# Two batches of small matmuls in an RWKV chain write to another PSUM bank of a two-layer hybrid decoder kernel

## The chip, the cores and the metric

The kernel runs on one core of one Trainium2 chip. The metric is the device time in microseconds of one execution, lower is better. Times of three runs are given, and one further execution was profiled; all views of the trace are of that one.

## The reference, cut to what matters

Two layers of a decoder trunk on 512 tokens of width 1024, in float32. Each layer normalises x, multiplies it by one large matrix, and hands the columns to three token mixers: latent attention (MLA), attention with a forget gate (FOX), and RWKV-7. Their outputs are gated, projected, merged and projected once more.

```python
for l in range(DEPTH):
    h = rmsnorm(x, norm_g[l])
    p = h @ w_in[l]
    (c_q, c_kv, k_r, gate_a, fq, fk, fv, ff, gate_b, shift_cols, gate_c, merge_cols) = split_cols(p, IN_SIZES)
    o_a = mla_branch(c_q, c_kv, k_r, gate_a, ...)
    o_b = fox_branch(fq, fk, fv, ff, gate_b, ...)
    r, k, v, wl, al = split_cols(shifted, RWKV_SIZES)
    o_c = rwkv_branch(r, k, v, wl, al, gate_c, ...)
    merged = sigmoid(g_a)*(o_a @ w_pa[l]) + sigmoid(g_b)*(o_b @ w_pb[l]) + sigmoid(g_c)*(o_c @ w_pc[l])
    x = x + merged @ w_out[l]

def rwkv7_scan(r, w, k, v, kk, a):      # per head, state S is 64 x 64
    sa = einsum('bhvk,bhk->bhv', state, -kk_t)
    state = state * w_t + sa * (kk_t * a_t) + v_t * k_t
    y_t = einsum('bhvk,bhk->bhv', state, r_t)
```

## The kernel before

**The dense part.** A projection is 8 blocks of 128 rows of weights against h. Weights and h are each split into a high and a low part, so a block is three matmuls of 128x512 (`mm3`, lines 816 to 818) and a projection 24, all adding up in one PSUM bank with the tag `acc`. A weight block comes by DMA (`raw`), ACT or DVE copies its high part (line 684), and DVE or POOL subtracts to get the low part (line 696).

**The PSUM banks.** There are eight: three for `acc`, two for `wk` (attention scores and small products of the attention's preparation), and one each for `xk`, `ch` and `av`. The preparation of an RWKV head pair uses `xk`, and `ch` beside it for the products called At. The RWKV chain of a pair uses `ch`. The attention's values use `av`.

**RWKV.** The recurrence is computed in chunks of 64 tokens, for four head pairs per layer, so eight times in the kernel. For each pair:

- The preparation ends with a sum over heads in `xk` (lines 712 and 713) that DVE turns into `bv` (line 1012). Then come two halves of At: 8 matmuls of 64x128 each (line 1018, 16 rows in the trace), alternately into `xk` and `ch`, and after each half two DVE products with a mask (line 1022) that empty the two banks. Then an inverse is built, partly on POOL, and ends with two rounds of small matmuls in `xk` (lines 1061 and 1067).
- The chain takes four batches of 64x64 blocks, written by the helper `one` (line 1099). The first, called here **the M batch**, alternates between R in `ch` and M in `xk`. The second, **the T batch**, alternates between U in `ch` and T in `xk`; it reads R and M, which ACT or DVE copied from PSUM in between. Two more batches in `ch` follow, then six dependent steps of the state (line 1139 on PE, line 1140 on DVE), and the output (lines 1146 and 1150).

**What sets the order.** Five generators per layer emit the work: `p` (RWKV preparation), `c` (RWKV chain), `y` (attention), `z` (merge gates) and `m` (merge). `weave` takes steps from them in a given order; a generator that yields "wait" lets another go first. A function `plan` then lists the emitted instructions engine by engine, with costs and due times, and that list is the order on the chip: each engine works through its own list in that order. `kernel` plans several times, with random shifts of the due times, and keeps the plan with the lowest score. So an edit in one place can move instructions everywhere.

**The rule for banks.** Tiles of one tag take its banks in the order in which they were emitted. `plan` puts the first instruction of a tile behind the first instruction of the tile emitted before it, and behind the last use of the tile that had the bank:

```python
        for x, y in zip(ns, ns[1:]):
            if uses[x][0] < uses[y][0]:
                ops[uses[y][0]].after.setdefault(uses[x][0], False)
        for x, y in zip(ns, ns[slots[tag]:]):
            for k in uses[x]:
                if k < uses[y][0]:
                    successors[k].append(uses[y][0])
```

A projection is emitted only while fewer than three `acc` tiles are open (`open_`).

Of the kernel before, what the change touches and what calls it, by code (L numbers as in the profile page):

```python
# [79 lines left out]

BUFS = {"tx": 8, "ty": 4, "sm": 1, "pp": 2, "raw": 4, "w": 6}
MB = ["wk", "wk", "av", "xk", "ch", "wk", "av", "xk"]
MARGINS = (1.7, 1.5)
SLACK = 1.2
WIRE, AHEAD = 250, 1500
ROUNDS = 3
WINDOW = 3413
SEARCH, JITTER = 12, 2000
PB = {"acc": 3, "wk": 2, "xk": 1, "ch": 1, "av": 1}
DRY = {"raw": 4, "w": 6, "acc": 1}  # L90

# [480 lines left out]
def build(tc, x_t, wpk, wsm, wv, vec, cst, out, order_of=None, pick={}, queues=None, margin=2.0):  # L572
    dry = order_of is None
# [34 lines left out]
    def PS(tag, z=""):  # L608
        b = PB[tag]
        if dry and tag == "acc":  # L610
            b, tag = DRY["acc"], tag + z
        return psum.tile([128, 512], F32, name=tag, tag=tag, bufs=b)
# [12 lines left out]
    def beside(insts):  # L625

        for a, b in zip(insts, insts[1:]):
            order(b, a)
# [6 lines left out]
    def size(ap):  # L635
        return math.prod(q[1] for q in ap.ap[1:])
# [33 lines left out]
    def any_of(costs, emit):  # L670

        key = (stream[0], turn[stream[0]])
        turn[stream[0]] += 1
        q = pick.get(key, costs[0][0])
        flex[emit(q).ins.name] = (key, costs)

    def in_psum(ap):
        return tags[ap.tensor.name][0] == "ps"

    def copy(dst, src, first=ACT):  # L680
        n, p = size(src), in_psum(src)
        costs = [(ACT, (52 if p else 94) + 0.833 * n), (DVE, 68 + n / (0.96 if p else 1.92))]
        any_of(costs if first == ACT else costs[::-1],
               lambda q: act.activation(dst, src, AF.Copy) if q == ACT else dve.tensor_copy(dst, src))  # L684

    def fill(dst, v):
        n = size(dst)
        any_of([(POOL, 34 + 0.836 * n), (DVE, 8 + n / 0.96)], lambda q: (dve if q == DVE else gp).memset(dst, v))
# [73 lines left out]
    for l in range(L):  # L762
# [57 lines left out]
        open_ = [0]  # L820
# [251 lines left out]
        def rwkv_chain(p, ops):  # L1072
# [25 lines left out]
            chunks = lambda tag="ch": PS(tag).rearrange("p (c t) -> p c t", t=64)  # L1098
# [5 lines left out]
                for h, hs in enumerate(HS):  # L1104
                    copy(KT[SH[h], i:8:2, :], ps[es, :, hs])
            yield
            pr, pm = chunks(), chunks("xk")
            beside([one(*a) for c in range(8) for h in range(2) for a in
                    ((pr[SH[h], c, :], At[HS[h], h, c, 0:64], VSA[HS[h], c, HS[h]]),
                     (pm[SH[h], c, :], W[SH[h], c, :], KT[SH[h], c, :]))])  # L1110
            copy(R, pr)
            copy(M, pm)
            yield
            pu, pt = chunks(), chunks("xk")
            beside([one(*a) for c in range(8) for h in range(2) for a in
                    ((pu[SH[h], c, :], W[SH[h], c, :], R[SH[h], c, :]),
                     (pt[HS[h], c, :], M[SH[h], c, :], KBn[SH[h], c, HS[h]]))])
# [7 lines left out]
            for h, hs in enumerate(HS):  # L1125
                fill(KBn[hs, :, SH[h]], 0.0)
                dve.tensor_tensor(KBn[hs, :, hs], pt[hs], C["ident"][hs, hs].unsqueeze(1).broadcast_to([64, 8, 64]),
                                  op=ALU.add)
            yield
            ps = chunks()  # L1130
            for c in range(8):
# [61 lines left out]
        def rwkv_chains():  # L1193
            for p in range(4):
                while len(ready) <= p:
                    yield "wait"
                yield from rwkv_chain(p, ready[p])
                done[0] += 1
# [602 lines left out]
```

## Time and profile before

| | |
|---|---|
| three runs | 1364.81 us median, 1363.15 to 1365.7 |
| the profiled execution, its own time | 1366.35 us |
| its span, first to last instruction | 1364.6 us |
| granted TensorE clock, mean | 0.996 of full speed |
| busy: PE, DVE, ACT, POOL | 97%, 78%, 68%, 30% of the span |
| PE idle | 1364.6 - 1318.9 = 45.7 us |

PE is TensorE, PEld its weight loads, DVE VectorE, ACT ScalarE, POOL GpSimd. A matmul's row shows its whole passage through the array, about 0.40 us for 128x512, while the next may start 0.23 us after it; so a PE that is "busy" can still be waiting a little between starts, and the idle time is only the part of the waiting that shows.

### The profile page before, as it was taken

The numbers are of one execution on the slowest core, as the hardware profiler recorded it, in microseconds if no ns is written. First come the engines' busy times: TensorE is split into PE (matmuls) and PEld (weight loads), VectorE is DVE, ScalarE is ACT, GpSimd is POOL, SyncE is SP. The second block draws the span as 40 slices with busy tenths as digits, with TensorE's granted clock in tenths as the row PEclk, the third lists the DMA queues.
The fourth block names the chain that finished last, engine by engine and source line by source line (L and its number), as shares of the span: only waits on it lengthen the run. The fifth ranks groups of instructions, "written<-read, shape, count | busy, mean of one in ns | idle before, by whom it ended". The sixth has DMA issues, their size and how long they took to land.

```text
span 1364.6 us, 25008 instructions
## 1 busy us (share of the span) xinstructions
PE 1318.9 (97%) x8532; PEld 1049.0 (77%) x8532; DVE 1070.8 (78%) x2430; ACT 934.5 (68%) x1905; POOL 407.5 (30%) x794
## 2 busy tenths in 40 slices
PE   7999999999999999999999999999999999999998
PEld 6777778878777887688877777777776777777787
DVE  8867887788897777977788689878887688848883
ACT  8658677676877775854556767766787588857631
POOL 1245443116211611320021443531254043503210
PEclk9999999999999999999999999999999989999999
DMA  5443233233232342465535333323234333334662
GB/s 176 131 130 103 95 95 92 73 120 102 75 120 75 120 125 71 150 191 180 174 90 164 99 103 100 104 82 91 81 92 107 98 94 106 93 117 124 194 218 97
DMA packets 114623, 158.67 MB, mean 116 GB/s; under 512 B 36544, under 2 KB 44608, under 8 KB 114496
## 3 DMA queue, kind: packets, MB, share of 16 engines
q1 hardware_dynamic: 114496, 157.08, 38.0%
q8 instruction: 67, 1.10, 0.3%
q14 instruction: 60, 0.49, 0.1%
HBM read 128.72 MB, written 28.31 MB: 115 GB/s over the span
## 4 chain that ended last, share of the span: by engine, by line
PE 71%; DVE 15%; ACT 11%; issue 3%; DMA 0%; SPq 0%; DVEq 0%; ACTq 0%
PE acc L817 16%; PE acc L816 16%; PE acc L818 16%; PE wk L1248 3%; PE ch L1099 2%; DVE w L696 2%; ACT w L684 1%; PE av L1260 1%; PE av L1262 1%; DVE qk L684 1%; PE wk L816 1%; PE av L1261 1%; DVE PP L696 1%; PE xk L1018 1%; PE wk L818 1%
## 5 line engine op out<-in xcount | busy, mean ns | idle before, releaser
L816 PE MATMUL acc<-hh,w 128*128 128x512 f32 x1008 | 374.4, 404 | 16.1 <-ACT hh L684 9.0
L818 PE MATMUL acc<-hh,w 128*128 128x512 f32 x1008 | 370.8, 403 | 2.8 <-DVE w L696 2.8
L817 PE MATMUL acc<-hl,w 128*128 128x512 f32 x1008 | 369.7, 402 | 1.3 <-DVE hl L696 1.1
L684 ACT ACTIVATE w<-raw 128x256 fp32r<-128x256 f32 (+1 forms) x544 | 216.6, 412 | 199.1 <-PE acc L818 162.7
L696 DVE TENSOR_TENSOR w<-raw,w 128x256 fp32r<-128x256 f32 x569 | 245.5, 444 | 73.4 <-ACT w L684 69.1
L816 PEld LDWEIGHTS acc<-hh,w 128*128 128x128 f32 x1008 | 189.1, 190 | 60.5 <-ACT hh L684 9.9
L696 POOL TENSOR_TENSOR w<-raw,w 128x256 fp32r<-128x256 f32 (+1 forms) x131 | 116.4, 895 | 399.5 <-ACT w L684 251.8
L818 PEld LDWEIGHTS acc<-hh,w 128*128 128x128 f32 x1008 | 188.7, 189 | 42.6 <-DVE w L696 4.8
L817 PEld LDWEIGHTS acc<-hl,w 128*128 128x128 f32 x1008 | 189.3, 189 | 41.1 <-DVE hl L696 3.1
L1041 POOL TENSOR_TENSOR W<-W,NL 128x60 f32<-128x60 f32 (+24 forms) x248 | 87.6, 353 | 83.4 <-DMA NL<-d 53.0
L1043 POOL TENSOR_TENSOR W<-W 128x60 f32<-128x60 f32 (+24 forms) x248 | 94.2, 380 | 18.1
L1248 PE MATMUL wk<-qk 96*128 96x512 f32 (+9 forms) x320 | 95.8, 319 | 3.5 <-DVE PP L696 2.4
L696 DVE TENSOR_TENSOR PP<-wk,PP 128x512 fp32r<-128x512 f32 (+3 forms) x128 | 61.0, 484 | 17.0 <-ACT PP L684 16.1
L1248 PEld LDWEIGHTS wk<-qk 128*128 128x128 f32 (+2 forms) x320 | 59.9, 189 | 17.5 <-DVE PP L696 6.6
L684 DVE CAST w<-raw 128x256 fp32r<-128x256 f32 (+1 forms) x156 | 46.9, 307 | 31.2 <-PE acc L818 26.0
L1223 DVE CUSTOM_DVE_ANT_0 wk<-wk,cmask 128x128 f32<-128x128 f32 (+3 forms) x128 | 61.4, 498 | 6.2 <-PE wk L1222 5.6
L684 ACT ACTIVATE PP<-wk 128x512 fp32r<-128x512 f32 (+3 forms) x122 | 52.0, 435 | 9.8 <-PE av L1262 5.9
L1249 DVE TENSOR_TENSOR wk<-wk,dmask 128x128 f32<-128x128 f32 x128 | 37.1, 292 | 21.9 <-PE wk L1248 21.3
L1253 ACT ACTIVATE wk<-wk,ncum 128x512 f32<-128x512 f32 (+1 forms) x64 | 31.3, 494 | 21.6 <-DVE wk L1249 21.4
L1253 ACT ACTIVATE wk<-wk 128x512 f32<-128x512 f32 (+1 forms) x64 | 26.9, 423 | 27.9 <-DVE wk L1249 27.4
L817 PE MATMUL acc<-mKR,w 128*128 128x512 f32 x128 | 46.0, 397 | 0.0
L684 ACT ACTIVATE KV<-ch 64x256 f32<-64x256 f32 (+2 forms) x65 | 32.7, 503 | 18.0 <-PE ch L1150 10.7
(532 smaller groups left out, 2872.2 us busy)
## 6 DMA issues: line engine op xcount, KB each, us to landing
raw<-wpk SPq DMA_DIRECT2D x326, 256.0 KB, 2.7
thd<-zth SPq DMA_DIRECT2D x48, 256.0 KB, 2.1
tx<-thd SPq DMA_DIRECT2D x44, 256.0 KB, 3.4
tx<-odr SPq DMA_DIRECT2D x22, 256.0 KB, 3.8
raw<-wpk SPq DMA_DIRECT2D x32, 128.0 KB, 2.2
NL<-d SPq DMA_DIRECT2D x32, 128.0 KB, 2.9
odr<-sg SPq DMA_DIRECT2D x14, 256.0 KB, 2.4
sum<-thd SPq DMA_DIRECT2D x10, 256.0 KB, 2.8
```

Of the source, the lines that this page charges most:

```text
L684: lambda q: act.activation(dst, src, AF.Copy) if q == ACT else dve.tensor_copy(dst, src))
L696: any_of(costs, lambda q: (dve if q == DVE else gp).tensor_tensor(dst, a, b, op=op))
L816: pe.matmul(ps, wh, xh, start=first, stop=False)
L817: pe.matmul(ps, wh, xl, start=False, stop=False)
L818: pe.matmul(ps, wl, xh, start=False, stop=last)
L1041: gp.tensor_tensor(tv, WL[:, 0:m, s:s + 1].broadcast_to([128, m, n]), NL[:, s:s + 1, s + 1:32].broadcast_to([128, m, n]), op=ALU.mult)
L1043: gp.tensor_tensor(WL[:, 0:m, s + 1:32], WL[:, 0:m, s + 1:32], tv, op=ALU.add)
L1099: one = lambda *a: pe.matmul(*a, start=True, stop=True)
L1223: dve.tensor_tensor_reduce(out=ps[:, 0:n], in0=ps[:, 0:n], in1=cmask[:, 512 - n:512], scale=1.0, scalar=NEG, op0=ALU.add, op1=ALU.max, acc ...
L1248: pe.matmul(pv, t[rows, k, js], t[rows, q, q0:512], start=i == 0, stop=i == len(passes) - 1)
L1249: dve.tensor_tensor(ps[:, js], ps[:, js], dmask, op=ALU.add)
L1253: act.activation(pv, pv, AF.Exp, scale=A["scale"], bias=b)
```

## The change

The M tile and the T tile move from the bank `xk` to the ring of three `acc` banks. The chain counts each as an open `acc` tile (`open_`), and waits at emission while three are open. The planner's list of margins gets a third entry, and each planning makes 8 random attempts in place of 12.

```diff
-MARGINS = (1.7, 1.5)
+MARGINS = (1.5, 1.7, 1.5)
...
-SEARCH, JITTER = 12, 2000
+SEARCH, JITTER = 8, 2000
...
-            pr, pm = chunks(), chunks("xk")
+            while not dry and open_[0] >= PB["acc"]:
+                yield "wait"
+            open_[0] += 1
+            pr, pm = chunks(), PS("acc", "c").rearrange("p (c t) -> p c t", t=64)
             beside([one(*a) for c in range(8) for h in range(2) for a in
                     ((pr[SH[h], c, :], At[HS[h], h, c, 0:64], VSA[HS[h], c, HS[h]]),
                      (pm[SH[h], c, :], W[SH[h], c, :], KT[SH[h], c, :]))])
             copy(R, pr)
             copy(M, pm)
+            open_[0] -= 1
             yield
-            pu, pt = chunks(), chunks("xk")
+            while not dry and open_[0] >= PB["acc"]:
+                yield "wait"
+            open_[0] += 1
+            pu, pt = chunks(), PS("acc", "c").rearrange("p (c t) -> p c t", t=64)
...
+            open_[0] -= 1
             yield
```

The program has 7092 matmuls before and after. The new plan lists them in another order from the first projections on. Two places are shown, both of the third head pair of the second layer, on PE. The names are those of the tiles, with their numbers; every `acc` tile read from `hh` or `hl` is a projection, `wk` tiles written at line 1222 (line 1230 in the changed file) are attention scores.

The first place, before: the end of the M batch (`ch_12845`, `xk_12846`) and the start of the T batch (`ch_12886`, `xk_12887`).

```order
L1099 MATMUL ch_12845<-KV_12592,At_11290 64x64
L1099 MATMUL xk_12846<-KR_11254,W_11997 64x64
L712 MATMUL wk_13193<-PP_13194,bd_95 128x512
L816 MATMUL acc_13352<-hh_7485,w_13355 128x512
L713 MATMUL wk_13193<-PP_13194,bd_95 128x512
L817 MATMUL acc_13352<-hl_7486,w_13355 128x512
L816 MATMUL acc_13376<-hh_7485,w_13379 128x512
L818 MATMUL acc_13352<-hh_7485,w_13355 128x512
L817 MATMUL acc_13376<-hl_7486,w_13379 128x512
L1099 MATMUL ch_12886<-At_11290,W_11997 64x64
L1099 MATMUL xk_12887<-KV_12592,At_11290 64x64
```

Five projection matmuls and two of a sum stand between the two batches.

The same place in the changed kernel: the M batch is `ch_12692` and `acc_12693`, the T batch `ch_12750` and `acc_12751`. The first rows are the scores before the M batch, the last ones the first projections after the T batch.

```order
L1230 MATMUL wk_12744<-qk1_12513 128x384
L1230 MATMUL wk_12747<-qk1_12513 128x512
L1099 MATMUL ch_12692<-KV_12165,At_11306 64x64
L1099 MATMUL acc_12693<-KR_11273,W_11706 64x64
...
L1099 MATMUL ch_12750<-At_11306,W_11706 64x64
L1099 MATMUL acc_12751<-KV_12165,At_11306 64x64
...
L816 MATMUL acc_12815<-hh_7485,w_12818 128x512
L816 MATMUL acc_12844<-hh_7485,w_12847 128x512
L817 MATMUL acc_12815<-hl_7486,w_12818 128x512
```

The T batch follows the M batch with nothing between, and no projection starts before the T batch has. (The left-out rows are the rest of the two batches.)

The second place, before: from the sum that feeds `bv` (`xk_11263`) to the first half of At (`xk_11291`, `ch_11292`).

```order
L713 MATMUL xk_11263<-PP_11264,bd_95 128x512
L817 MATMUL acc_11571<-hl_7486,w_11574 128x512
L1262 MATMUL av_11303<-PP_11348,Vh_9231 128x128
L818 MATMUL acc_11571<-hh_7485,w_11574 128x512
L816 MATMUL acc_11571<-hh_7485,w_11592 128x512
L1222 MATMUL wk_11429<-qk1_8177 128x256
L1222 MATMUL wk_11432<-qk1_8177 128x384
L817 MATMUL acc_11571<-hl_7486,w_11592 128x512
L1018 MATMUL xk_11291<-KR_11254,KB0_11253 128x128
L1018 MATMUL ch_11292<-KR_11254,KB0_11253 128x128
```

Four projection matmuls, two scores and one product of the values stand between.

The same place in the changed kernel, which here runs on into the rows of the first place: the sum is `xk_12491`, the halves are `xk_12533` with `ch_12534` and `xk_12545` with `ch_12546`.

```order
L818 MATMUL acc_12416<-hh_7485,w_12475 128x512
L713 MATMUL xk_12491<-PP_12492,bd_95 128x512
L1230 MATMUL wk_12668<-qk0_12379 128x256
L1230 MATMUL wk_12689<-qk0_12379 128x384
L1230 MATMUL wk_12728<-qk0_12379 128x512
L1018 MATMUL xk_12533<-KR_12482,KB0_12481 128x128
L1018 MATMUL ch_12534<-KR_12482,KB0_12481 128x128
...
L1230 MATMUL wk_12738<-qk1_12513 128x128
L1230 MATMUL wk_12741<-qk1_12513 128x256
L1018 MATMUL xk_12545<-KR_12482,KB0_12481 128x128
L1018 MATMUL ch_12546<-KR_12482,KB0_12481 128x128
```

The row of `acc_12416` is the last of that projection and the last of any until `acc_12815`: the sum, both halves of At, the M batch and the T batch stand in one stretch with scores alone between them.

## Rows read from the trace of the kernel before

**Rows 1.** The page, its first part: busy us, share of the span, instructions.

```profile
PE 1318.9 (97%) x8532; PEld 1049.0 (77%) x8532; DVE 1070.8 (78%) x2430; ACT 934.5 (68%) x1905; POOL 407.5 (30%) x794
```

**Rows 2.** The page, the chain that ended last: shares of the span by engine.

```profile
PE 71%; DVE 15%; ACT 11%; issue 3%; DMA 0%; SPq 0%; DVEq 0%; ACTq 0%
```

**Rows 3.** Windows of the span: busy us (instructions) by engine, granted clock, DMA share, GB/s.

```profile
536.10:584.80 48.70, 45.61 (x261) 35.69 (x261) 42.92 (x99) 34.77 (x70) 14.62 (x15) 1.00 0.41 130
1218.40:1267.10 48.70, 46.20 (x284) 36.49 (x281) 41.12 (x95) 33.65 (x68) 16.40 (x15) 1.00 0.40 123
```

**Rows 4.** Line 1099, 1209.3 to 1216.8 us: duration ns min/median/max, first and last start.

```profile
L1099 PE MATMUL ch<-KV,At x32: 218/218/267, 1209.4 to 1210.4; 64*64 64x64 f32 x32
L1099 PE MATMUL ch<-At,W x32: 218/218/267, 1212.5 to 1213.4; 64*64 64x64 f32 x32
```

**Rows 5.** Timeline of ACT, 1209 to 1216 us: start, us, instruction, idle before.

```profile
1210.71 0.60 ACT L684 ACTIVATE At<-ch 128x512 f32<-128x512 f32 x1 [0.77 <-PE xk L1099]
1211.20 0.59 ACT L684 ACTIVATE At<-xk 128x512 f32<-128x512 f32 x1
```

**Rows 6.** Groups on PE, 1209.6 to 1212.4 us: busy us, mean ns, idle before.

```profile
L816 PE MATMUL acc<-hh,w 128*128 128x512 f32 x3 | 1.1, 430 | 0.0
L817 PE MATMUL acc<-hl,w 128*128 128x512 f32 x3 | 0.9, 392 | 0.0
```

**Rows 7.** Timeline of DVE, 857 to 862.5 us.

```profile
856.69 0.67 DVE L1012 SCALAR_TENSOR_TENSOR bv<-xk,vp 128x512 f32<-128x512 f32 x1
...
858.86 0.69 DVE L1022 TENSOR_TENSOR At<-xk,amask 128x512 f32<-128x512 f32 x1
859.46 0.68 DVE L1022 TENSOR_TENSOR At<-ch,amask 128x512 f32<-128x512 f32 x1
...
861.60 0.69 DVE L1022 TENSOR_TENSOR At<-xk,amask 128x512 f32<-128x512 f32 x1
```

**Rows 8.** Timeline of PE, 857.6 to 861.5 us: from one half of At to the next.

```profile
857.66 0.37 PE L1018 MATMUL xk<-KR,KB 64*128 64x128 f32 x1
...
858.55 0.27 PE L1018 MATMUL ch<-KR,KB 64*128 64x128 f32 x1
...
860.41 0.37 PE L1018 MATMUL xk<-KR,KB 64*128 64x128 f32 x1
```

**Rows 9.** The same stretches as windows, columns as in rows 3.

```profile
857.70:860.40 2.70, 2.70 (x29) 2.34 (x28) 2.24 (x6) 1.70 (x6) 0.00 (x0) 1.00 0.51 150
1209.40:1212.50 3.10, 3.10 (x75) 2.45 (x75) 0.76 (x2) 1.62 (x4) 0.00 (x0) 1.00 0.40 142
```

**Rows 10.** Lines 1061 and 1067, 1199 to 1206 us, columns as in rows 4.

```profile
L1061 PE MATMUL xk<-NL,At x32: 191/191/212, 1199.2 to 1200.1; 32*32 32x32 f32 x32
L1067 PE MATMUL xk<-W,NL x32: 191/191/212, 1201.6 to 1202.1; 32*32 32x32 f32 x32
```

**Rows 11.** Timeline of ACT, 1199.5 to 1206 us.

```profile
1202.35 0.78 ACT L684 ACTIVATE W<-xk 32x256 f32<-32x256 f32 x2 [0.30 <-PE xk L1067]
```

**Rows 12.** Timeline of PE, 1220 to 1222.6 us: steps of the state.

```profile
1220.17 0.33 PE L1139 MATMUL ch<-At,KV 128*128 128x64 f32 x2
1220.31 0.71 PE L817 MATMUL acc<-hl,w 128*128 128x512 f32 x2
1220.86 0.63 PE L818 MATMUL acc<-hh,w 128*128 128x512 f32 x2
1221.33 0.33 PE L1139 MATMUL ch<-KR,KV 128*128 128x64 f32 x2
```

**Rows 13.** Timeline of DVE, 1220 to 1223.5 us.

```profile
1220.54 0.28 DVE L1140 SCALAR_TENSOR_TENSOR KR<-ch,lam,At 128x64 f32<-128x64 f32 x1
```

**Rows 14.** Windows around the one fall of the clock in mid-kernel, columns as in rows 3.

```profile
1105.00:1110.00 5.00, 3.91 (x20) 2.69 (x18) 4.78 (x8) 4.75 (x11) 3.11 (x4) 1.00 0.22 59
1110.00:1115.00 5.00, 4.19 (x14) 3.18 (x15) 4.07 (x7) 4.01 (x10) 0.20 (x1) 0.54 0.36 97
1115.00:1120.00 5.00, 5.00 (x23) 4.10 (x23) 3.65 (x9) 4.04 (x9) 1.29 (x1) 0.78 0.87 270
```

## The prediction

> **What bounds the kernel now.** I read the page first: PE is busy 97% of the span, DVE 78%, ACT 68% [rows 1]. The chain that ended last says the same from the other side: 71% of it is work on PE, 15% DVE, 11% ACT, and no DMA to speak of [rows 2]. So time is lost or won on PE. Its idle time is small, 45.7 us, and about 6 us of that lie in the two windows where the attention of a layer runs out, 3.1 us in 536 to 585 and 2.5 us in 1218 to 1267 [rows 3]. What matters for this change is how idle time is kept small: wherever a chain of small steps crosses from PE to another engine and back, the list of PE has projection matmuls in between. The two stretches that the change touches show it. Between the M batch and the T batch at 1209 us lie seven projection matmuls, six of them in [rows 6], and PE is busy for all 3.10 us, and between two halves of At at 857 us PE is busy for all 2.70 us [rows 9].
>
> **What the change does to the work.** Nothing is added on PE: 7092 matmuls before and after, with the same shapes. DVE, ACT and POOL trade some splits. So the term that counts is the order. In the change's list I counted the projection matmuls between M and T for the eight head pairs. Before: 2, 211, 11, 5, 5, 245, 5, 7. After: 0, 0, 3, 0, 0, 0, 0, 0. The reason can be read in the bank rule. M and T now stand in the ring of `acc`. A projection emitted after them may not start before T has started, and T waits for R and M, which go through ACT. The projection that was open finishes, and then PE has nothing of that kind to do, even where a bank is empty. In seven of the eight pairs the whole stretch up to the T batch is without projections, and in four of them it also takes in the sum for `bv` and both halves of At.
>
> **The price of one M to T.** The M batch starts at 1209.4 and its last row at 1210.4 [rows 4]; with 0.1 us until the next matmul can start, a batch takes 1.16 us. The two copies on ACT begin at 1210.71 and end at 1211.79 [rows 5], and with about 0.05 us to tell PE the T batch could start at 1211.85, 2.45 us after M. It started at 1212.5, because the projections had not ended: the wait was hidden altogether. Without projections PE gets 2.45 us, less its own 1.16 us, less what other work stands between. Where one of the two copies goes to DVE (two of eight after the change) it is 0.5 us less.
>
> **Four stretches with the halves of At.** The steps, from the sum's last matmul: 0.4 us until it is out (a 128x512 matmul's row), then `bv` starts, 1.0 us until the first half starts (856.69 to 857.66, [rows 7, 8]); 2.75 us until the second half, since its banks must first be emptied by the two products with the mask, 858.86 to 860.14; and 2.5 us more until the second pair of products has ended (861.60, plus the same 0.60 and 0.68), when `ch` is free for the M batch [rows 7, 8]. Then 2.45 us to T and 1.16 us of T. Sum 10.25 us. PE's own work in the stretches is 2 x 1.1 for the halves (857.66 to 858.75 by the rows' pace, [rows 8]), 2 x 1.16 for the batches, and the other rows of the list at 0.23 us for 512 columns, the pace at which two matmuls follow each other [rows 12], less for narrower ones: 2.4, 1.4, 2.8 and 1.4 us. Together 6.8, 5.9, 7.2 and 5.8 us, so 3.4, 4.4, 3.0 and 4.5 us are lost, 15.3 in all. Before the change these hops lose about half a microsecond each, by the starts, that I take off: 13.3 us. The bounds: if DVE and ACT are never behind other work, each path is some 8.5 us and the loss 6 us; if DVE first works through the scores that stand among these rows in its list, some 11.5 us, and the loss 18 us. I take the middle, because it is what the rows at 857 us show with DVE busy 2.24 of 2.70 us.
>
> **The other pairs.** In the last pair of the first layer the stretch takes in the two rounds of the inverse: 2.4 us from line 1061 to line 1067 [rows 10], 1.55 us until ACT has copied W (1201.6 to 1203.13, [rows 10, 11]), then 2.45 and 1.16: 7.55 us, against 4.95 us of PE's own work, so 2.6 us lost. The remaining three pairs have only M to T: 2.45 - 1.16 less 0.33, 1.21 and 1.13 us of other work, 1.2 us together.
>
> **The steps of the state.** Before, at least four projection matmuls stand between two steps; after, 18 of the 40 gaps hold three. A step at 1220.17 gives DVE its start at 1220.54, which ends at 1220.82, so 0.7 us are needed [rows 12, 13]; three projections and the step itself take 0.83 us, enough if DVE is prompt. Where it is late, up to 0.2 us are lost. I take 1 us in all, between 0 and 4.
>
> **What comes back.** While PE waits, DVE and ACT go on with the splits of weights, up to six tiles ahead, so some later waits of PE shrink. They can give back at most what PE idles for weights, a few of the 45.7 us. I take 4 us, from 0 to 10. The shifted splits and six more table loads on ACT are hidden: ACT is idle a third of the span [rows 1].
>
> The sum is 13.3 + 2.6 + 1.2 + 1 - 4 = 14.1 us. Against the profiled execution's 1366.35 us that is 1380.5; the median of the runs is 1.5 us lower, 1364.81, so I expect **1379 us**.
>
> **Rivals.** *The freed `xk` pays.* The chains come much earlier in the change's list: the last output of the first layer stands after 31% of PE's matmul work, where before it stood after 39%. With `xk` shared no more the preparation need not wait, all four pairs are done early, and the merge has its operand when the attention runs out. If the 5.6 us of idle time in those two windows [rows 3] and as much hidden waiting around them go, and the stretches above cost little because PE would have waited there anyway, the time is 1354 us. It decides if the stretches cost less than 11 us. For it speaks that these windows are the idlest outside the start; against it that projections last only a little longer into the attention's end after the change, and that every gap I counted became shorter, none longer. 23%.
>
> *PE's waiting is only moved.* DVE and ACT are close behind PE (DVE 41 to 43 us of 48.7 in [rows 3]); if they set the pace over tens of microseconds, each stretch lets them catch up and all of the loss returns: 1365 us. Against it: the weight tiles are few, so they can't run far ahead. 14%.
>
> *The clock falls.* [...] Against it: the batches of small matmuls keep PE busy in between. 11%. [...]
>
> The forecast itself, slower by 4 to 25 us without falls of the clock, gets 52%.
>
> **How the numbers follow.** A measurement of this kernel can tell about 0.2%, 2.7 us. Faster is the first rival, 23%; same is the second, 14%; slower is the forecast and the third, 63%. Cases of both signs hold much of the chance, so the range goes from 1356 us, which takes in the first rival's nearer half, to 1394 us, the highest losses or the falling clock; it leaves out the other half of the first rival, some 12%, and a clock that falls more often, some 5%. The forecast's own range is 1369 to 1390.
>
> **What would show it.** Right: PE's idle time rises to 55 us or more; PE waits at line 1099 for ACT's copies `At<-ch` and `At<-acc`, at line 1018 for DVE's `bv` and At, and the scores of line 1230 for DVE; M to T starts are near 2.45 us apart and no `acc` projection stands in the stretch. Wrong: M to T takes 2 us or less, or the stretches lose what I say and the time is still not longer; then the waits for weights must have shrunk by as much, or the windows at the attention's end must show PE idle less. A wait of PE for weights right behind a stretch would show that nothing comes back. The clock's share in the windows decides the third rival.

## The result, and the profile after

| | before | changed |
|---|---|---|
| median | 1364.76 us (1363.15 to 1365.7) | 1400.72 us (1396.59 to 1404.29) |
| ratio, 95% interval | | 1.0256, 1.0242 to 1.0270 |
| profiled execution, its span | 1366.35, 1364.6 us | 1396.59, 1394.8 us |

The change makes the kernel 2.6% slower. The direction was forecast; the size was not: 36 us in place of 14, and 6.7 us above the upper end of the range.

The page of the changed kernel, with the rows that answer to [rows 1, 2], and the granted clock in 40 slices of the span (tenths of full speed):

```profile
PE 1338.8 (96%) x8532; PEld 1062.1 (76%) x8532; DVE 1065.4 (76%) x2411; ACT 947.2 (68%) x1911; POOL 413.0 (30%) x813
...
PEclk9999999999998999999999999899999999999999
...
PE 60%; DVE 13%; ACT 9%; issue 3%; POOL 2%; DMA 1%; SPq 0%; POOLq 0%; ACTq 0%; DVEq 0%
```

PE's idle time went from 45.7 to 56.0 us (1394.8 less 1338.8), and PE's work in the chain that ended last fell from 71% to 60%. PE is also *busy* 20 us longer for the same matmuls (1338.8 against 1318.9 us): it ran slower for a part of the time, with a mean granted clock of 0.984 where it was 0.996.

Windows of the changed kernel: first two of the stretches without projections, then the two ends of the attention (which answer to [rows 3]), then around five falls of the clock, each time a window ahead of the fall and the fall itself. Columns as in [rows 3].

```profile
168.20:181.30 13.10, 9.60 (x175) 7.46 (x176) 10.77 (x26) 7.81 (x17) 3.13 (x6) 0.87 0.22 51
1092.30:1106.80 14.50, 11.07 (x170) 8.36 (x169) 11.52 (x31) 8.95 (x16) 7.64 (x6) 0.76 0.49 147
566.00:614.00 48.00, 47.92 (x227) 38.58 (x227) 31.50 (x85) 32.34 (x71) 8.69 (x10) 1.00 0.37 112
1262.00:1310.00 48.00, 48.00 (x228) 39.08 (x227) 34.64 (x89) 31.06 (x68) 0.82 (x1) 1.00 0.43 134
165.00:172.20 7.20, 4.26 (x29) 2.98 (x27) 7.12 (x11) 5.68 (x15) 6.33 (x9) 1.00 0.30 78
172.20:175.60 3.40, 3.40 (x16) 2.35 (x14) 3.29 (x9) 1.49 (x3) 0.00 (x0) 0.50 0.08 28
262.00:267.80 5.80, 2.24 (x16) 1.45 (x17) 5.71 (x6) 5.69 (x10) 5.02 (x6) 1.00 0.29 90
267.80:274.60 6.80, 6.80 (x88) 5.62 (x88) 5.80 (x18) 1.49 (x3) 1.26 (x1) 0.50 0.33 117
418.50:424.80 6.30, 4.13 (x56) 3.12 (x55) 6.11 (x15) 6.13 (x13) 3.14 (x5) 1.00 0.32 65
424.80:438.50 13.70, 13.10 (x211) 9.87 (x206) 8.44 (x27) 9.36 (x18) 0.00 (x0) 0.50 0.16 55
872.00:878.80 6.80, 5.62 (x28) 3.66 (x27) 6.77 (x16) 6.39 (x14) 3.42 (x4) 1.00 0.17 52
878.80:889.00 10.20, 10.06 (x108) 8.43 (x107) 7.67 (x24) 4.87 (x9) 1.26 (x1) 0.50 0.22 66
1091.00:1097.20 6.20, 3.66 (x17) 1.96 (x17) 6.20 (x14) 6.05 (x11) 5.89 (x5) 1.00 0.76 248
1097.20:1104.00 6.80, 6.78 (x79) 5.50 (x78) 5.73 (x17) 2.91 (x6) 2.97 (x3) 0.50 0.42 128
```

Three things are to be seen. First, before four of these falls PE was busy 39% to 66% of the window, while DVE was busy 97% to 100% of it: PE waits, DVE is full. Before the one at 878.8 us DVE was as full, but PE was busy 83%. DVE is full only in the first part of a stretch: over the whole it is busy 82% (10.77 of 13.10 us) at 168 us and 79% (11.52 of 14.50 us) at 1092 us. Second, the granted clock went to 0.50 right behind. There are six such falls in mid-kernel, 44.3 us at the lower level together. These five stand in or next to the stretches; the sixth, at 114.2 us, does not (ahead of it PE was busy 54%, DVE 73%). The trace of before has two, the 6.8 us of [rows 14] and 3.4 us at 38.6 us. Third, in these windows at the ends of the attention PE now idles 0.1 us where it idled 5.6 us.

Timeline of PE in the changed kernel at two of these places, from the last projection to the first half of At:

```profile
166.95 0.39 PE L818 MATMUL acc<-hh,w 128*128 128x512 f32 x1
168.22 0.50 PE L712 MATMUL xk<-PP,bd 128*128 128x512 f32 x1 [0.88 <-ACT PP L684]
169.83 0.50 PE L713 MATMUL xk<-PP,bd 128*128 128x512 f32 x1 [1.11 <-DVE PP L696]
171.28 0.37 PE L1018 MATMUL xk<-KR,KB 64*128 64x128 f32 x1 [0.95 <-DVE bv L1012]
...
1092.31 0.50 PE L713 MATMUL xk<-PP,bd 128*128 128x512 f32 x1
1093.52 0.39 PE L1230 MATMUL wk<-qk 128*128 128x256 f32 x1 [0.70 <-DVE Vl L696]
1094.86 0.44 PE L1230 MATMUL wk<-qk 128*128 128x384 f32 x1 [0.96 <-DVE ty L1231]
1096.12 0.49 PE L1230 MATMUL wk<-qk 128*128 128x512 f32 x1 [0.82 <-DVE ty L1231]
1096.67 0.49 PE L1018 MATMUL xk<-KR,KB 64*128 64x128 f32 x2
```

The waits begin earlier than the prediction's path did: the two matmuls of the sum wait for the high and the low half of their operand. And the scores, which the prediction counted as cover, wait themselves (0.70, 0.96 and 0.82 us), for DVE to empty one of the two `wk` banks. What DVE does meanwhile, at the second place:

```profile
1092.79 0.67 DVE L696 TENSOR_TENSOR Vl<-wk,Vh 128x512 fp32r<-128x512 f32 x1
1093.39 1.15 DVE L939 SCALAR_TENSOR_TENSOR tx<-tx 128x512 f32<-128x512 f32 x1
1094.46 0.28 DVE L1231 CUSTOM_DVE_ANT_0 wk<-wk,cmask 128x128 f32<-128x128 f32 x1
...
1094.67 1.00 DVE L940 SCALAR_TENSOR_TENSOR vp<-tx,vp 128x512 f32<-128x512 f32 x1
...
1095.94 0.68 DVE L1012 SCALAR_TENSOR_TENSOR bv<-xk,vp 128x512 f32<-128x512 f32 x1
```

The sum had ended by 1092.81 (the timeline's 1092.31 and 0.50), `bv` starts at 1095.94. DVE goes through its own list, back to back. But two entries of it, 2.15 us, are `bv`'s own: `bv` reads the sum and `vp`, and in the second layer lines 939 and 940 write `vp` first. In the trace of before `vp` is just as late, 6 us behind the sum:

```profile
850.32 0.40 PE L713 MATMUL xk<-PP,bd 128*128 128x512 f32 x1
...
855.89 0.68 DVE L940 SCALAR_TENSOR_TENSOR vp<-tx,vp 128x512 f32<-128x512 f32 x1
...
856.69 0.67 DVE L1012 SCALAR_TENSOR_TENSOR bv<-xk,vp 128x512 f32<-128x512 f32 x1
```

M to T. Line 1099 in the changed kernel from 1102.5 to 1107 us (columns as in [rows 4]): 2.4 us between the first starts, with the M batch at the lower clock (a median of 311 ns in place of 218).

```profile
L1099 PE MATMUL ch<-KV,At x32: 218/311/366, 1102.8 to 1104.3; 64*64 64x64 f32 x32
...
L1099 PE MATMUL ch<-At,W x32: 218/218/267, 1105.2 to 1106.6; 64*64 64x64 f32 x32
```

Over the eight pairs these first starts lie 1.9, 3.2, 2.4, 3.7, 3.1, 2.5, 2.4 and 3.5 us apart, where 2.45 us were forecast, or 0.5 less with a copy on DVE, as in the first pair. The 3.2, 3.7 and 3.1 us begin in falls of the clock, as the 2.4 us shown do; in the last pair attention matmuls stand between.

The waits of PE in the changed kernel, by line and by what it waited for (us in total, times, longest), without the two largest, which are the start of each layer:

```profile
PE wk L1256 <- DVE PP L696: 4.6, 9, 1.5
PE wk L1230 <- DVE ty L1231: 3.6, 5, 1.0
PE xk L713 <- DVE PP L696: 3.6, 3, 2.1
...
PE xk L1018 <- DVE bv L1012: 2.4, 2, 1.5
PE ch L1099 <- ACT At L684: 2.3, 3, 0.8
```

Since idle time shows only part of the waiting, I also took for every matmul the time to the next start, less the pace of its shape (the lower third of such times in the trace of before). By that measure PE loses 133.4 us in the profiled execution of before and 163.9 us in that of the change. The stretches lose:

| stretch, us | forecast | measured | of it at the lower clock |
|---|---|---|---|
| 168 to 181 (sum, halves of At, M, T) | 3.4 | 7.8 | 1.8 |
| 265 to 277 (the same) | 4.4 | 9.0 | 4.1 |
| 877 to 886 (the same; small MLA matmuls ahead of M) | 3.0 | 6.5 | 4.7 |
| 1092 to 1107 (the same) | 4.5 | 9.2 | 4.0 |
| 419 to 435 (inverse, M, T) | 2.6 | 10.0 | 5.6 |
| 992 to 998, 1162 to 1170 (M, T) | 1.2 | 4.6 | 0 |
| sum | 19.1 | 47.1 | 20.2 |

Against that stand 16.6 us that PE loses less in the rest of the kernel (47.1 less 30.5). What the kernel before lost at the same hops, 2 us by the prediction, is part of them.

### The profile page after: what moved, and what is told of

It is laid out like the page before. It is cut to its first block, busy times and chain, and to the rows that moved or that the text cites. A ratio compares the mean times of both kernels' runs of the same rounds, so it can differ in the third digit from the quotient of the medians.

```text
span 1394.8 us, 24957 instructions
## 1 busy us (share of the span) xinstructions
PE 1338.8 (96%) x8532; PEld 1062.1 (76%) x8532; DVE 1065.4 (76%) x2411; ACT 947.2 (68%) x1911; POOL 413.0 (30%) x813
## 4 chain that ended last, share of the span: by engine, by line
PE 60%; DVE 13%; ACT 9%; issue 3%; POOL 2%; DMA 1%; SPq 0%; POOLq 0%; ACTq 0%; DVEq 0%
PE acc L816 14%; PE acc L818 14%; PE acc L817 14%; PE wk L1256 2%; PE ch L1099 1%; DVE PP L696 1%; PE wk L1230 1%; DVE w L696 1%; POOL W L1043 1%; POOL W L1041 1%; PE xk L1018 1%; PE wk L816 1%; PE av L1268 1%; ACT qk L684 1%; PE wk L817 1%
## 5 line engine op out<-in xcount | busy, mean ns | idle before, releaser
L696 DVE TENSOR_TENSOR w<-raw,w 128x256 fp32r<-128x256 f32 (+1 forms) x553 | 239.7, 444 | 102.6 <-ACT w L684 96.9
L696 POOL TENSOR_TENSOR w<-raw,w 128x256 fp32r<-128x256 f32 x147 | 129.7, 886 | 531.4 <-ACT w L684 365.9
L1256 PE MATMUL wk<-qk 96*128 96x256 f32 (+10 forms) x320 | 97.1, 325 | 4.8 <-DVE PP L696 4.6
L1043 POOL TENSOR_TENSOR W<-W 128x60 f32<-128x60 f32 (+24 forms) x248 | 85.6, 345 | 18.6
L684 DVE CAST w<-raw 128x256 fp32r<-128x256 f32 x156 | 47.2, 305 | 38.5 <-PE acc L818 32.4
L1231 DVE CUSTOM_DVE_ANT_0 wk<-wk,cmask 128x256 f32<-128x256 f32 (+3 forms) x128 | 61.4, 500 | 9.5 <-PE wk L1230 8.9
L684 ACT ACTIVATE PP<-wk 128x256 fp32r<-128x256 f32 (+3 forms) x122 | 51.8, 434 | 4.2 <-PE av L1270 1.6
L1230 PE MATMUL wk<-qk 96*128 96x384 f32 (+7 forms) x128 | 44.8, 377 | 4.7 <-DVE ty L1231 3.6
L1268 PE MATMUL av<-PP,Vh 128*128 128x512 f32 (+3 forms) x128 | 43.5, 340 | 1.8 <-ACT do L684 0.8
L1270 PE MATMUL av<-PP,Vh 128*128 128x512 f32 (+3 forms) x128 | 42.1, 329 | 0.0
```

The lines of the kernel that those rows point to most:

```text
L696: any_of(costs, lambda q: (dve if q == DVE else gp).tensor_tensor(dst, a, b, op=op))
L1043: gp.tensor_tensor(WL[:, 0:m, s + 1:32], WL[:, 0:m, s + 1:32], tv, op=ALU.add)
L1230: pe.matmul(ps[:, 0:n], t[sr, A["sq"], 128 * i:n], t[sr, 2, 0:n], start=True, stop=True)
L1231: dve.tensor_tensor_reduce(out=ps[:, 0:n], in0=ps[:, 0:n], in1=cmask[:, 512 - n:512], scale=1.0, scalar=NEG, op0=ALU.add, op1=ALU.max, acc ...
L1256: pe.matmul(pv, t[rows, k, js], t[rows, q, q0:512], start=i == 0, stop=i == len(passes) - 1)
L1268: pe.matmul(av[:, q0:512], vh, ph, start=j == 0, stop=False)
```

## The experiments

Theory A: the ring's order keeps projections away, PE waits uncovered, and the clock falls on top. Rivals: the planner's numbers or its luck (B), a bank less for projections (C), DVE and ACT set the pace anyway (D), the freed `xk` pays (E).

**The planner's numbers.** The changed kernel with `MARGINS` and `SEARCH` of before, and the other way round:

```diff
-MARGINS = (1.5, 1.7, 1.5)
+MARGINS = (1.7, 1.5)
-SEARCH, JITTER = 8, 2000
+SEARCH, JITTER = 12, 2000
```

> The changed kernel, planned with the margins and the number of random attempts of the kernel before. Theory A (bank order): M and T in the ring of acc keep projections from starting, so the list of PE has no projections in seven or eight stretches, PE waits there for ACT and DVE, and the clock falls in some of them. The new list has no projection between M and T in five of eight pairs and stretches without any of up to 9 us of work, longer than in the changed kernel: 1390 to 1415 us. Theory B (the planner's numbers): the two margins and the number of attempts made the worse plan, so the time goes back to 1360 to 1370 us.

> The kernel before, planned with the three margins and the eight attempts of the changed one. Its list keeps 1 to 243 projections between M and T. Theory A: 1360 to 1370 us, and no fall of the clock beyond the few of before. Theory B: near 1400 us.

Measured: 1411.83 us (ratio to before 1.0344, 1.0328 to 1.0359) and 1363.75 us (0.9994, 0.9984 to 1.0004). B falls: the numbers make nothing worse, and the banks do it under either.

**Other random numbers**, for both rules:

```diff
-    draw = random.Random(1)
+    draw = random.Random(2)
```

> The changed kernel with other random numbers in the planner. Its list has five stretches without projections in place of eight, and projections between M and T again in half of the pairs. Theory A: a plan's time follows its stretches, so 1375 to 1395 us, still slower than before by 0.8% or more, since the rule holds for every draw. Theory B (the changed kernel had a bad draw): 1368 us or less.

> The kernel before, planned with other random numbers: how far two draws of one rule lie apart. Theory A: cover is kept by the rule in every draw (2 to 233 projections between M and T), so 1360 to 1372 us. If the kernel before is a lucky draw, 1375 us or more, and then the loss of the change is partly this luck.

Measured: 1386.21 us (1.0144, 1.0117 to 1.0170) for the change, 1376.36 us (1.0085, 1.0071 to 1.0099) for before. The second lies above what A gave and in the range that was named for a lucky draw. So a draw is worth some 10 us either way, and the kernel before is a good one. The three plans under the old banks take 1364, 1365 and 1376 us, the three under the new ones 1386, 1401 and 1412: the groups do not meet. By their means, 1368 and 1400 us, the banks cost 31 us, and some 5 of the 36 us are the draw.

**Cover alone.** The plan of before on every engine; in seven places the projections on PE move behind the small batch:

```diff
+LAST = [(1107, 1182), (1504, 1539), (2748, 2819), (3853, 3884), (4767, 4840), (5847, 5918), (6336, 6408)]
+        at = [i for i, k in enumerate(q) if type(insts[k]).__name__ == "InstMatmult"]
+        for a, b in LAST if len(at) > 5000 else ():
+            rows = [q[i] for i in at[a:b]]
+            rows.sort(key=lambda k: insts[k].outs[0].bass_ap.tensor.name.startswith("acc"))
+            for i, k in zip(at[a:b], rows):
+                q[i] = k
```

> The kernel before with its own plan on all engines, M and T in xk; only the list of PE is changed in seven places: the 2 to 8 projection matmuls between M and T of five pairs, and the 6 and 14 between the sum and the second half of At of two pairs, move behind T or the second half. Theory A: this cover is what counts. The five M to T lose about 1.2 us each where only small work is left and less where scores stand, the two others 1.4 and 2.6 us: 6 to 10 us in all if the clock holds, up to 20 us with a fall or two; 1370 to 1385 us. Theory D (DVE and ACT set the pace, PE's waits are only moved): 1363 to 1367 us.

Measured: 1374.75 us (1.0057, 1.0042 to 1.0072), 8 us more, with a mean clock of 0.994 to 0.998. The last M to T, where nothing else stands between (line 1099 is line 1100 here):

```profile
L1100 PE MATMUL xk<-KR,W x32: 218/218/267, 1213.4 to 1214.4; 64*64 64x64 f32 x32
...
L1100 PE MATMUL ch<-At,W x32: 218/218/267, 1215.3 to 1216.7; 64*64 64x64 f32 x32
...
L1100 PE MATMUL xk<-KV,At x32: 218/218/267, 1215.8 to 1216.7; 64*64 64x64 f32 x32
```

2.4 us from the rows of M to those of T, as forecast from [rows 4, 5]. But the T batch opens with U (`ch<-At,W`), which reads only the first of the two copies, and does so 2.0 us after M; its end is as forecast, since every second row waits for the other copy. By starts, four of the five M to T lose 0.8 to 1.2 us each, the fifth, with scores between, nothing. D falls for these hops: a few uncovered microseconds on PE stay in the time.

**The ring's order alone.** M and T stay in `acc`, but each tile's first instruction is a small one that waits for nothing, and `plan` pairs the batches by the instruction behind it:

```diff
+            bank = PS("acc", "c")
+            pe.matmul(bank[:, 0:64], CR["bd"], CR["bd"][:, 0:64], start=True, stop=True)
-            pr, pm = chunks(), PS("acc", "c").rearrange("p (c t) -> p c t", t=64)
+            pr, pm = chunks(), bank.rearrange("p (c t) -> p c t", t=64)
...
-    firsts = {l[0]: n for n, l in uses.items() if n in psum}
+    early = lambda k: ops[k].array and ops[k].ins[0][0] == ops[k].ins[1][0] and ops[k].ins[0][0][:2] == "bd"
+    firsts = {l[1 if early(l[0]) else 0]: n for n, l in uses.items() if n in psum}
```

> The changed kernel with one small extra matmul (64 columns of a constant) as the first instruction in the bank of M and one in the bank of T, overwritten by the batch: 16 matmuls, about 1 us of PE. The rule for banks looks only at a tile's first instruction, so projections emitted behind M and T may now start before the batches do. Theory A: projections stand between M and T again (1 to 54 in the new list), PE idles 25 us less than in the changed kernel, the falls of the clock in mid-kernel are two at most, and the time is 1355 to 1378 us. Theory C (a bank less for projections): M and T hold their banks even longer, projections wait for banks, so the time stays at 1390 us or more.

The same with `random.Random(2)`:

> The kernel with the small early matmuls in the banks of M and T, planned with other random numbers. Its list has 2 to 60 projections between M and T, and only three stretches without projections over 2.5 us, the longest 3.7 us. Theory A (cover is all): two falls of the clock in mid-kernel at most and 1360 to 1370 us, near the kernel before. If a bank less for the projections or the early chains cost something of their own, it stays at 1375 to 1385 us.

Measured: 1380.23 us (1.0112, 1.0097 to 1.0127) and 1371.19 us (1.0044, 1.0031 to 1.0056), both just above what A gave. PE's idle time in the second one is 1368.5 - 1323.6 = 44.9 us:

```profile
PE 1323.6 (97%) x8548; PEld 1054.9 (77%) x8548; DVE 1075.5 (79%) x2448; ACT 944.3 (69%) x1918; POOL 376.8 (28%) x771
```

The clock does not recover as far as A said. The second draw (mean clock 0.994) keeps three falls of 3.4 us in mid-kernel (at 708, 875 and 1138 us), the first (0.991) four, where two at most were expected; and in the first PE idles 50.1 us, 6 us less than in the changed kernel and not 25.

Even so this is the strongest case for A: M and T hold their banks longer than in the changed kernel, and 15 to 21 us (first draw against first, second against second) come back. As the cause of most of the loss C falls with it. Against the kernel before with the same random numbers 15 us remain in the first draw, and the second is 5 us faster.

**M alone, T alone.** In the first T is back in `xk`, in the second, with the same edit, M:

```diff
-            while not dry and open_[0] >= PB["acc"]:
-                yield "wait"
-            open_[0] += 1
-            pu, pt = chunks(), PS("acc", "c").rearrange("p (c t) -> p c t", t=64)
+            pu, pt = chunks(), chunks("xk")
```

> Only M stands in the ring of acc, T is back in xk. Theory A: 4 to 187 projections stand between M and T again, but stretches without projections of 3 to 8 us remain ahead of M in six or seven places: about half of the loss, 1372 to 1390 us, with fewer and shorter falls of the clock than in the changed kernel. Theory C: the projections lose the bank for a shorter time, so 1370 to 1385 as well, but then PE waits at the first matmul of projections for DVE to empty a bank. Theory B (the planner's numbers, which are those of the changed kernel): 1400 us.

> Only T stands in the ring of acc, M is back in xk. In the new list five stretches without projections of more than 2.5 us of work are left, where the changed kernel has eight, and 213, 23 and 209 projections stand between M and T of three pairs. Theory A: the loss goes with these stretches and with the falls of the clock in them: 1370 to 1390 us. Theory C (a bank less for the projections): T holds its bank longer than M, so most of the loss stays, 1390 us or more.

Measured: 1427.38 us (1.0453, 1.0437 to 1.0468) and 1385.20 us (1.0137, 1.0120 to 1.0154). For T this is what A gave. For M it is far off: one tile in the ring is worse than two. PE in the kernel with M alone, at the worst place:

```profile
1239.40 0.80 PE L712 MATMUL wk<-PP,bd 128*128 128x512 f32 x1 [3.44 <-ACT PP L684]
...
1244.62 1.08 PE L1080 MATMUL ch<-cs,KB 128*128 128x128 f32 x4 [3.14 <-DVE KV L684]
1246.39 1.12 PE L1085 MATMUL ch<-cs,vp 128*128 128x128 f32 x4 [0.69 <-ACT KV L684]
...
1249.14 1.12 PE L1102 MATMUL ch<-cs,KR 128*128 128x128 f32 x4 [1.00 <-ACT KV L684]
1251.90 0.37 PE L1099 MATMUL ch<-KV,At 64*64 64x64 f32 x1 [1.64 <-ACT KR L684]
```

No projection stands here; three rounds of transposes and copies that lead up to M are uncovered, and the granted clock is 0.50 for all of it, 1239.4 to 1254 us. So it isn't the number of tiles in the ring that counts. That it is instead how long the first instruction of one has to wait, and that the ring's rule keeps projections away here, as it did for both tiles together, is argued and not shown: no run takes M alone apart.

**M and T in the ring of the scores.**

```diff
-            pr, pm = chunks(), PS("acc", "c").rearrange("p (c t) -> p c t", t=64)
+            pr, pm = chunks(), chunks("wk")
-            pu, pt = chunks(), PS("acc", "c").rearrange("p (c t) -> p c t", t=64)
+            pu, pt = chunks(), chunks("wk")
```

(The waits for `open_` go with both.)

> M and T in the two banks of the scores (wk): xk is freed for the preparation as in the changed kernel, and the ring of acc holds only projections and merges. The new list has 5 or 6 projections between M and T in five of eight pairs, the chains end even earlier than in the changed kernel, and behind them stand six stretches of 4 to 12 us of attention without projections in each layer. Theory A (cover decides): the pairs cost nothing, but the attention's end has lost its cover, 1385 to 1430 us with falls of the clock there. Theory E (a freed xk pays, and only the ring of acc spoils it): 1364 us or less.

Measured: 1557.41 us (1.1403, 1.1384 to 1.1422), far beyond what A gave. Two windows in which PE's list has only the attention and its preparation:

```profile
424.70:452.00 27.30, 22.89 (x76) 17.86 (x77) 13.60 (x39) 15.47 (x36) 0.00 (x0) 0.50 0.13 43
...
1206.80:1226.60 19.80, 14.50 (x49) 10.01 (x49) 11.19 (x35) 12.06 (x22) 0.00 (x0) 0.66 0.09 27
```

E falls in this form: the preparation has `xk` to itself and the chains end earliest of all, but then the projections are spent early too, the attention behind has no cover, and the clock is at 0.50 for all of the first window (mean over the span 0.921).

**The clock.** The changed kernel's plan and order, with extra matmuls that nothing waits for at places where PE idled in the stretches. The table gives the place in PE's list, the bank they write, and how many:

```diff
+FILL = {718: ('h1', 3), 719: ('h1', 5), 720: ('h1', 4), 748: ('m0', 3), 780: ('t0', 3),
...
+        def pad(ps, kind):
+            if queues is not None:
+                junk[kind].append([])
+                j = kind + str(len(junk[kind]) - 1)
+                junk[kind][-1] += [pe.matmul(ps, CR["bd"], hh[:, 0, :], start=True, stop=True).ins
+                                   for i, c in FILL.values() if i == j for _ in range(c)]
```

> The changed kernel with its own plan and order, and 70 extra matmuls of 128x512 on constant and finished data, put at the places where PE idles in six of the stretches without projections (1 to 8 at a place, sized by the idle time there). They write a bank that the next batch overwrites and nothing waits for their result. Theory A with the clock as the larger part: PE does no more useful work, but the falls of the clock at 172, 268, 425 and 1097 us (30.7 us at half speed together) go, those at 114 and 879 us, which are left alone, stay; 1382 to 1393 us, though 70 more matmuls are in the list. Theory W (the waits alone cost, the clock is a side effect of little price): the time stays at 1396 us or rises by what the extra matmuls delay, up to 1415 us.

> As the kernel with 70 extra matmuls, now with 86: at 418 us they write the bank of M in place of that of the transposes, for which they had to wait, the first stretch of the second pair gets 16 in place of 8, and the halves of At at 879 us get 8. Theory A with the clock as the larger part: the falls at 271, 422 and 882 us (3.4, 13.7 and 6.8 us there) shrink or go too, the one at 114 us stays; 1384 to 1392 us against 1394 with 70. Theory W (the clock has little price): 1394 us or more, since the list has 3.7 us more work than with 70.

Measured: 1394.08 us (1.0206, 1.0189 to 1.0223) and 1393.44 us (1.0203, 1.0185 to 1.0220). Neither theory's range holds it; the truth lies between. Windows of the kernel with 70 extra matmuls:

```profile
168.20:181.00 12.80, 12.58 (x196) 9.33 (x196) 11.63 (x27) 8.73 (x19) 3.42 (x7) 1.00 0.21 53
1092.40:1105.50 13.10, 12.03 (x185) 8.60 (x184) 11.53 (x31) 8.99 (x16) 7.71 (x6) 1.00 0.54 166
417.20:436.50 19.30, 16.90 (x232) 12.42 (x231) 13.97 (x39) 13.85 (x26) 3.18 (x5) 0.65 0.10 22
```

Where PE was kept going the falls are gone: PE busy 12.58 of 12.80 us where it was 9.60 of 13.10, the clock 1.00 where it was 0.87; and 12.03 of 13.10 us where it was 11.07 of 14.50, the clock 1.00 where it was 0.76. So in these two stretches it is PE's waiting that brings them. The windows do not begin and end at the same instructions; from the sum's second matmul to the one behind the T batch the first stretch takes 10.0 us in place of 11.3, the second 13.1 in place of 14.5:

```profile
169.83 0.50 PE L713 MATMUL xk<-PP,bd 128*128 128x512 f32 x1 [1.11 <-DVE PP L696]
...
181.08 0.39 PE L1268 MATMUL av<-PP,Vh 128*128 128x256 f32 x1
```

This is the changed kernel, and the one with 70 extra matmuls (line 713 is 715 there, 1268 is 1286):

```profile
170.08 0.50 PE L715 MATMUL xk<-PP,bd 128*128 128x512 f32 x1
...
180.07 0.38 PE L1286 MATMUL av<-PP,Vh 128*128 128x256 f32 x1
```

So at full clock these two are 1.3 and 1.4 us shorter; the rest of their length is the chain of hops, which the extra matmuls leave as it was. At 417 us the extra matmuls had to wait for a bank themselves, and the fall stayed; at 271.5 us 3.4 of 6.8 us stayed. With 86 of them, and another bank at 418 us, 3.4 us of that fall are left, and the falls at 271 and 882 us are gone. But there are others in their place, at 42, 936 and 1216 us (3.4, 6.8 and 3.4 us), so 20.5 us stand at the lower level where 27.3 us stood with 70, and the extra matmuls nearly take what that brings.

A second measure of the clock's price costs no edit. The four runs of the changed kernel are one program, and differ in how much the clock fell:

| span, us | mean clock | (1 - clock) x span |
|---|---|---|
| 1394.8 | 0.984 | 22.3 |
| 1396.7 | 0.981 | 26.5 |
| 1401.2 | 0.978 | 30.8 |
| 1402.5 | 0.976 | 33.7 |

7.7 us of span for 11.4 us lost to the clock: 0.7 us for each. Straight lines through the runs of most other kernels here give 0.4 to 0.7 (before 0.44 over 38 runs, T alone 0.68); that of the early instructions in the second draw gives 1.0, and three whose runs hardly differ in clock give no usable line. The changed kernel loses 28 us to the clock on average, before 4: if the line holds that far, the difference costs 10 to 17 us, say 14. The 70 extra matmuls agree with the lower end: 15 us less lost to the clock, 6.6 us less time. So in most of these runs a microsecond lost to the clock costs less than a microsecond of span. That PE is often waiting anyway in such a stretch is a likely reason, not a shown one.

## Why the prediction was wrong

**Right: the mechanism and its direction.** Projections behind M and T in the ring cannot start, PE's list has stretches without cover, and PE waits there for `bv`, for At and for the copies, as named. The experiments with the early instruction and with the moved projections show the two halves of this, the rule and the cover, one by one. The price of M to T held for T's own rows at full clock (2.4 us with the projections moved); the batch opens 0.45 us sooner and ends as forecast.

**Wrong: the path through the four stretches.** The prediction put 10.25 us between bounds of 8.5 and 11.5 us, "the middle, because it is what the rows at 857 us show with DVE busy 2.24 of 2.70 us". Its steps, from first start to first start, against the four stretches of the changed kernel (by their begin) and against two of them with 70 extra matmuls, at full clock:

| step, us | forecast | 168 | 265 | 877 | 1092 | 168, extra | 1092, extra |
|---|---|---|---|---|---|---|---|
| sum's last matmul to first half | 1.4 | 1.45 | 1.95 | 3.16 | 4.36 | 1.45 | 4.40 |
| to second half | 2.75 | 4.05 | 2.39 | 2.84 | 2.65 | 2.80 | 2.32 |
| to M | 2.5 | 2.67 | 3.40 | 4.54 | 3.45 | 2.66 | 2.93 |
| to the T batch | 2.45 | 1.86 | 3.23 | 3.14 | 2.44 | 1.99 | 1.98 |
| to the next matmul | 1.16 | 1.22 | 1.09 | 1.12 | 1.57 | 1.09 | 1.45 |
| sum | 10.25 | 11.25 | 12.06 | 14.80 | 14.47 | 9.99 | 13.08 |

The first step failed in the second layer: 3.2 and 4.4 us in place of 1.4, and 4.4 at full clock too. There `bv` starts behind `vp`, not behind the sum; the rows at 857 us begin with `bv` and cannot show it, and before the change other matmuls covered it. At 168 us, in the first layer, the path at full clock is as forecast (10.0 us, one copy on DVE). Most of what is more in the other steps goes with the clock, and at 877 us with the small MLA matmuls ahead of M: at full clock the stretch at 1092 us takes 8.7 us behind the first half, against a forecast of 8.9. The waits of the sum for its own operand, 0.9 and 1.1 us at 168 us and 2.1 us at 265 us, stood in no term of the forecast. Scores were counted as 0.23 us of cover each, but three at 1092 us wait for DVE themselves. In the inverse's stretch, 10.0 us in place of 2.6, 5.6 us fall into the lower clock and 1.4 us are a wait of line 1061 for DVE. In sum 47 us in place of 19, of which 20 at the lower clock.

**Wrong: the clock as an unlikely rival.** It had 11%, "the batches of small matmuls keep PE busy in between", and nothing of it stood in the sum. The falls by the stretches came before, during or right behind the first of those batches, four of them behind windows in which PE was busy 39% to 66%. By [rows 14] a fall costs up to 0.46 x 5 + 0.22 x 5 = 3.4 us; four of them, 13.6 us, agree with the 14 us by the runs' own scatter, but partly by luck: the falls by the stretches are five, and up to 13.7 us long. The trace of before, with two falls in mid-kernel (10.2 us at the lower level), does not show them as a habit; that of the changed kernel does, with six (44.3 us).

**Wrong: what comes back.** 4 us were expected; by starts it is 16.6 us. 5.5 us of it is the idle time at the ends of the attention, so the first rival's observation held, but paid little against the 47 us lost. For the rest I see no single place: it is spread over the kernel, with DVE and ACT further ahead. How much of it is the earlier chains and how much the catching up stays open.

Together, as an estimate: 36 us is about 14 for the clock and 22 for waits, where 14 were forecast for waits and the clock left out. The forecast with four such falls on top, 1379 + 13.6 = 1392.6 us, has the right parts, with the waits too small. That the kernel before is a good draw of its planner, worth perhaps 4 us against the mean of three, was not thought of at all.

No kernel tried is faster than the one before; before with the new planner's numbers is equal to it.

## What to carry to other kernels

A tile that must wait for a chain of hops should not share a ring, whose banks are handed out in order, with the tiles that serve as cover: one waiting first instruction holds back all tiles behind it, and an early first instruction that waits for nothing lifts that. When work without cover is priced, ask for every operand of each hop when it is written, not only for the one whose chain is followed: another that was covered before may now come last. Ask too what the fillers in between wait for themselves. And where a change makes PE wait in several microseconds at a time, as here, where five of the six falls came behind windows of 5.8 to 7.2 us in which PE was busy 39% to 66%, the clock's fall belongs in the forecast, not among the rivals.

## What was not expected of the hardware

PE counts as busy 3.40 of 3.40 us and 6.80 of 6.80 us in windows at a granted clock of 0.50: busy time alone hides a fall, and the 20 us more of busy time for the same matmuls is its mark on the page. And time lost to the clock was, in most kernels here, not lost one to one: 0.4 to 0.7 us of span for each.
